# A table of cumulative gates in DRAM: from one row per chunk and head to one row per direction and head

## The chip, the cores and the metric

The kernel runs on one core of a Trainium2 chip. Its time is the device time of one execution in microseconds, taken as the median of several runs. All data are float32 in DRAM; the matrix products of the projections run on float32r pairs of a high and a low part.

## The reference, cut to what matters

One hybrid layer: a bidirectional gated DeltaNet token mixer on 512 latent tokens with a prefix of 256 context tokens, then a mixture of 16 experts with 64 tokens each. Per head and direction the mixer needs the cumulative sum of the log gates within a chunk. It stands in the decay between two tokens of a chunk and in the decay of the query:

```python
gcum = jnp.cumsum(g, axis=-1)                       # (B, H, n, CHUNK)
diff = gcum[..., :, None] - gcum[..., None, :]
decay = jnp.where(incl, jnp.exp(jnp.where(incl, diff, 0.0)), 0.0)
a_low = jnp.where(strict, jnp.einsum('bhnid,bhnjd->bhnij', k_beta, k) * decay, 0.0)
sol = lax.linalg.triangular_solve(a_low + eye, rhs, lower=True, unit_diagonal=True)
att = jnp.einsum('bhnid,bhnjd->bhnij', q, k) * decay
q_dec = q * jnp.exp(gcum)[..., None]
...                                                 # scan over chunks, S_t = a_t (I - b_t k_t k_t^T) S_{t-1} + b_t k_t v_t^T
```

The kernel takes chunks of 128 tokens: 2 of context and 4 of latents, 6 in all, with 8 heads of 128 columns and 2 directions.

## The kernel before, in words

The program has two stages. In the first, up to about 630 us, PE computes the projections of head after head (lines 141 to 143, three products for each float32 one) and between them the small products of the DeltaNet heads. In the second it streams the weights of the 16 experts through a ring of buffers (`w`, line 636) and multiplies them with the tokens (lines 1580 and 1561).

The first stage is planned by hand: generators ask for an engine and a duration (`Ask`), the function `run` picks the next of them by its own reckoning of free times, and the instructions are recorded in that order. Each engine then runs its instructions strictly in the recorded order. `dma(nbytes, at)` is the planner's price of a transfer, and takes no account of how a transfer is cut. All loads and stores are issued by SP and share one queue over the 16 DMA engines, so a transfer waits for those issued before it.

`gates` computes the cumulative log gates of all heads at once. They are transposed to `gr`, 96 rows (direction, chunk, head) of 128 tokens, and stored to the table `grow_d` in DRAM (line 1022). From there each head reads rows back, with every row repeated over all 128 partitions:

- `head_a` (line 1060) loads one `ff` tile per direction, 6 chunks of 128 values on each partition, 384 KB. The address pattern comes from `grow`. POOL masks the tile (line 1065), ACT takes the exponential (line 105), DVE multiplies it with the products of the keys into `ct` (lines 1116, 1117) and sorts its diagonal blocks (`cd`), which go to DRAM as `bd` (line 1128).
- `invert` reads `bd` back as `lb` (line 1137) and inverts the blocks of 32 by 31 steps of two instructions on POOL (`tb` and `xb`, lines 1148 and 1150). The result goes out as `xd` (line 1153) and comes back as `cr` (line 1158). `head_b` goes on with it on DVE (`cx`, lines 1217 and 1218) and PE (line 1227 and after). Masks for a later head stand in the middle of these steps.
- `decay_q` (line 1290) loads one `qa` tile per direction, 4 latent chunks, 256 KB. ACT takes the exponential, POOL multiplies it with the queries (line 1298), and the scan's output product reads it (line 1348).

On the same engines run the short convolutions (DVE, line 283), the splitting of weights (ACT line 299, DVE and POOL line 303, from `wt<-in_win`, line 136), and the modulation: pieces `e<-in_wm` (line 344) that POOL, ACT and DVE reduce (lines 355 to 375) and PE sums up (lines 382 and 396). At the start the bias rows `gtm` (line 807) and `gtf` (line 809) are loaded in the same repeated manner from a row of `in_brow`.

The address pattern of the repeated loads before:

```python
def grow(d, h, c):
    return bass.AP(tensor=grow_d.tensor, offset=grow_d.offset + ((d * NCH + c) * H + h) * C,
                   ap=[[0, P], [H * C, NCH - c], [1, C]])
```

Of the kernel before, what the change touches and what calls it, by code (L numbers as in the profile page):

```python
# [11 lines left out]
F32 = mybir.dt.float32  # L12
# [7 lines left out]
P = 128  # L20
# [5 lines left out]
H = 8  # L26
C = 128
NC_CTX = CTX // C
NC_LAT = SEQ // C
NCH = NC_CTX + NC_LAT  # L30
# [19 lines left out]
def gdn_moe_kernel(ctx: ExitStack, tc: tile.TileContext, a, out):  # L50
# [889 lines left out]
    for b in range(2):  # L940
        for d in range(2):
# [3 lines left out]
    gt = qa[:, NCH * P:NCH * P + 4 * NCH * H].rearrange("p (c d t h) -> p c d t h", c=NCH, d=2, t=2)  # L945
    gc, gs, neg, egt = (ua[:, xw + i:xw + i + 2 * NCH * H].rearrange("p (d c h) -> p d c h", d=2, c=NCH)
                        for i in range(0, 8 * NCH * H, 2 * NCH * H))
    grow_d = tc.dram_tile([2 * NCH * H, C], F32, name="grow_d")

    def gates():  # L950
        abT = gp.tile([64, TOK], F32, tag="ff0_0", bufs=1, name="abT")
# [67 lines left out]
        v.tensor_copy(gr, pr)  # L1019
        give(sl, t2)  # L1020
        t2 = yield Ask("D", 0.5, t2)
        sy.dma_start(grow_d, gr)
        done["G", 0] = dma(1 << 16, t2)
        t = yield Ask("A", 0.4, t, table="exp")
        act("exp", neg, gc, AF.Exp)
# [17 lines left out]
        return pt  # L1043

    def grow(d, h, c):
        return bass.AP(tensor=grow_d.tensor, offset=grow_d.offset + ((d * NCH + c) * H + h) * C,
                       ap=[[0, P], [H * C, NCH - c], [1, C]])

    HALF = (range(0, 4), range(4, 6))

    def head_a(h):
# [5 lines left out]
        for d in range(2):  # L1057
            tf = yield Ask("D", 0.5, lambda: fin(("G", 0), ("T", h - 2)))
            f_ = head_tile(f"ff{d}_", h, [P, NCH, C])
            sy.dma_start(f_, grow(d, h, 0))  # L1060
            tf = dma(3 << 17, tf)
            ff.append(f_)
            sg = 1 if d == 0 else -1
            tf = yield Ask("G", 0.85, tf)
            g.affine_select(out=f_, in_=f_, pattern=[[0, NCH], [sg, C]], compare_op=OP.is_ge, fill=-1e30,
                            base=0, channel_multiplier=-sg)
# [215 lines left out]
    def decay_q(h):  # L1282
        x = hd[h]
        x["qd"] = []
        qds = qa[:, 1024:].rearrange("p (d t) -> p d t", d=2)
        t0 = []
        for d in range(2):
            t = yield Ask("D", 0.5, lambda: fin(("S0", h - 1), ("S1", h - 1)))
            qd = qds[:, d]
            sy.dma_start(qd.rearrange("p (c i) -> p c i", c=NC_LAT), grow(d, h, NC_CTX))  # L1290
            x["qd"].append(qd)
            t0.append(dma(1 << 18, t))
        for d in range(2):
            qd = x["qd"][d]
            t = yield Ask("A", av(SEQ), t0[d], table="exp")
            act("exp", qd, qd, AF.Exp)
            t = yield Ask("G", 1.25, lambda: None if fin(("q", h)) is None else max(t, fin(("q", h))))
            g.tensor_mul(qd, qd, x["q"])
            done[f"D{d}", h] = t
# [451 lines left out]
```

## Time and profile before

| | us |
|---|---|
| median of 3 runs | 1574.14 |
| lowest and highest | 1568.88, 1575.66 |
| the profiled execution, its own time | 1573.24 |
| its span, from the first to the last instruction | 1571.5 |

The profile is of one execution. A span is the time from the first to the last instruction; what lies around it is 1.7 us. The windows give the busy time of each engine in a stretch, the granted clock of PE and the busy share of the 16 DMA engines. The timeline gives one engine's instructions in order; in brackets stands how long the engine was idle ahead of one, and whose end released it. The chain of waits follows the program back from its last instruction.

### The profile page before, as it was taken

What the parts mean: (1) busy time and instruction counts of PE and PEld (TensorE: products, weight loads), DVE (VectorE), ACT (ScalarE), POOL (GpSimd) and SP (SyncE); (2) the same over time, 40 slices, a digit from 0 to 9 for tenths busy, and PEclk for the clock granted to TensorE, in tenths of its full rate; (3) what the DMA queues carried; (4) which work ended last, traced back from release to release, by engine and by line L of the source; (5) the groups of instructions that cost most, each with busy time, mean ns of one, the idle gap of its engine ahead of it and who ended that gap; (6) DMA issues with size and microseconds to landing.
All of it is one profiled execution on the core that took longest, in us unless ns stands there. A gap on an engine that the chain in (4) does not pass through costs nothing.

```text
span 1571.5 us, 20699 instructions
## 1 busy us (share of the span) xinstructions
PE 1374.7 (87%) x8058; PEld 752.6 (48%) x8058; DVE 721.5 (46%) x1545; ACT 405.3 (26%) x1038; POOL 381.0 (24%) x645
## 2 busy tenths in 40 slices
PE   5889898988986889999999989889889899899867
PEld 1677687766875766433434324224223323324314
DVE  7779896977995896222222222222222222222103
ACT  3356474655574533000000000000000000000012
POOL 2548866857657830000000000000000000000001
PEclk8889999999998999999999999999999999999979
DMA  8145443443453566899999999999999999999992
GB/s 347 54 135 142 135 114 91 117 130 95 133 122 72 205 243 248 364 426 426 425 426 425 425 426 426 427 425 425 426 425 426 426 425 426 425 426 426 425 426 109
DMA packets 112515, 480.12 MB, mean 306 GB/s; under 512 B 45505, under 2 KB 66209, under 8 KB 81826
## 3 DMA queue, kind: packets, MB, share of 16 engines
q1 hardware_dynamic: 112418, 478.81, 77.9%
q8 instruction: 63, 1.03, 0.3%
q14 instruction: 34, 0.28, 0.1%
HBM read 471.92 MB, written 6.86 MB: 305 GB/s over the span
## 4 chain that ended last, share of the span: by engine, by line
DMA 48%; PE 26%; DVE 14%; POOL 8%; issue 2%; ACT 1%; SPq 0%; DVEq 0%; POOLq 0%; ACTq 0%
DMA w<-in_wgu 25%; DMA w<-in_wd 13%; PE gu L1580 10%; PE dn L1561 4%; POOL xb L1150 3%; POOL tb L1148 3%; DMA cr<-xd 2%; DVE e L375 2%; PE gc L1561 2%; PE gc L1511 2%; DMA fg<-in_fg 1%; DVE wl L303 1%; DMA ff__690<-grow_d 1%; DMA ff__1139<-grow_d 1%; PE gc L1548 1%
## 5 line engine op out<-in xcount | busy, mean ns | idle before, releaser
L1580 PE MATMUL gu<-w,xsT 128*64 128x512 f32 x2044 | 472.9, 606 | 32.4 <-DMA w<-in_wgu 31.6
L1580 PEld LDWEIGHTS gu<-w,xsT 128*64 128x64 f32 x2044 | 138.4, 138 | 291.5 <-issue 239.4
L1667 POOL TENSOR_TENSOR hres<-acc,fg 128x256 f32<-128x256 f32 (+1 forms) x6 | 6.0, 1004 | 953.1 <-DVE acc L1655 953.0
L1561 PE MATMUL dn<-w,work 128*64 128x512 f32 x896 | 202.0, 600 | 25.2 <-DMA w<-in_wd 25.2
L1550 DVE TENSOR_TENSOR acc<-gc,acc 128x512 f32<-128x512 f32 x104 | 70.7, 690 | 299.5 <-PE gc L1548 299.5
L141 PE MATMUL pp<-uh,wh 128*128 128x512 f32 (+1 forms) x368 | 153.4, 417 | 1.7 <-ACT cz L265 1.7
L143 PE MATMUL pp<-uh,wl 128*128 128x512 f32 (+1 forms) x368 | 138.9, 377 | 3.8 <-DVE wl L303 2.9
L142 PE MATMUL pp<-ul,wh 128*128 128x512 f32 (+1 forms) x368 | 137.9, 375 | 0.0
L1561 PEld LDWEIGHTS dn<-w,work 128*64 128x64 f32 x896 | 62.4, 137 | 154.2 <-issue 116.8
L1148 POOL TENSOR_TENSOR tb<-lb,xb 96x126 f32<-96x126 f32 (+22 forms) x248 | 118.3, 477 | 65.8 <-DMA lb<-bd 48.6
L1150 POOL TENSOR_TENSOR xb<-xb,tb 96x126 f32<-96x126 f32 (+22 forms) x248 | 125.1, 504 | 19.4
L1532 ACT ACTIVATE work<-tr 128x512 f32<-128x512 f32 x14 | 8.4, 597 | 423.1 <-PE tr L1525 423.1
L1512 DVE TENSOR_SCALAR xsT<-gc,ffn 128x128 f32<-128x128 f32 x64 | 26.2, 410 | 154.1 <-PE gc L1511 154.1
L1542 ACT CAST yh<-work 64x512 fp32r<-64x512 f32 x28 | 17.3, 617 | 253.1 <-DVE work L1539 252.8
L143 PEld LDWEIGHTS pp<-uh,wl 128*128 128x128 f32 x368 | 74.7, 203 | 16.1 <-DVE wl L303 3.3
L141 PEld LDWEIGHTS pp<-uh,wh 128*128 128x128 f32 x368 | 75.1, 204 | 10.7 <-ACT cz L265 2.2
L142 PEld LDWEIGHTS pp<-ul,wh 128*128 128x128 f32 x368 | 75.3, 205 | 6.3
L1511 PEld LDWEIGHTS gc<-oneh,hres 128*128 128x128 f32 x512 | 64.5, 191 | 20.2 <-issue 18.3
L1511 PE MATMUL gc<-oneh,hres 128*128 128x128 f32 x512 | 69.2, 280 | 0.4 <-DVE oneh L1504 0.4
L375 DVE SCALAR_TENSOR_TENSOR e<-e,cs,e 128x128 f32<-128x128 f32 x133 | 66.0, 512 | 1.8
L1613 DVE TENSOR_TENSOR work<-gu,work 128x512 f32<-128x512 f32 x32 | 22.0, 692 | 80.9 <-PE gu L1580 79.7
L1548 PEld LDWEIGHTS gc<-yh,pgt 128*128 128x128 f32 x112 | 19.8, 186 | 82.0 <-issue 68.2
(443 smaller groups left out, 2042.7 us busy)
## 6 DMA issues: line engine op xcount, KB each, us to landing
w<-in_wgu SPq DMA_DIRECT2D x100, 2048.0 KB, 34.3
w<-in_wd SPq DMA_DIRECT2D x45, 2048.0 KB, 34.3
w<-in_wgu SPq DMA_DIRECT2D x55, 1024.0 KB, 31.9
w<-in_wd SPq DMA_DIRECT2D x22, 1024.0 KB, 31.8
e<-in_wm SPq DMA_DIRECT2D x32, 512.0 KB, 4.4
wt<-in_win SPq DMA_DIRECT2D x31, 512.0 KB, 4.6
w<-in_wdt SPq DMA_DIRECT2D x6, 2048.0 KB, 30.7
wm<-in_wm SPq DMA_DIRECT2D x3, 2048.0 KB, 14.6
```

The lines of the kernel that those rows point to most:

```text
L141: pe.matmul(pp, wh[:, k, :], uh[i][:, k, :], start=k == 0, stop=False)
L142: pe.matmul(pp, wh[:, k, :], ul[i][:, k, :], start=False, stop=False)
L143: pe.matmul(pp, wl[:, k, :], uh[i][:, k, :], start=False, stop=k == KT - 1)
L375: v.scalar_tensor_tensor(acc, wm[:, k], cs1[:, k, 0:1], acc, op0=OP.mult, op1=OP.add)
L1148: g.tensor_tensor(t_, lb[:, k + 1:, k:k + 1].to_broadcast([2 * NB, m, n_]), xb[:, k:k + 1, 0:n_].to_broadcast([2 * NB, m, n_]), OP.mult)
L1150: g.tensor_tensor(xb[:, k + 1:, 0:n_], xb[:, k + 1:, 0:n_], t_, OP.subtract)
L1511: pe.matmul(pg, hres[:, t, k * P:k * P + P], oneh[:, t].rearrange("p a b -> p (a b)"), start=t == 0, stop=t == NC_LAT - 1)
L1512: v.tensor_scalar(xsT[:, k, :], pg, ffn[:, 0, k:k + 1], ffn[:, 1, k:k + 1], op0=OP.mult, op1=OP.add)
L1548: pe.matmul(pcb, pgt[:, t, :], yh[:, dh], start=True, stop=True)
L1550: v.tensor_add(acc[t // 2][:, t % 2, cs], pcb, hres[:, t, cs] if first else acc[t // 2][:, t % 2, cs])
L1561: pe.matmul(pd[64 * g_:64 * g_ + 64], hs_[g_][i][:, cb, 64 * j:64 * j + 64], wcols(w, c0, w_), start=ft == 0, stop=ft == 15, tile_position ...
L1580: pe.matmul(gu[m][f // 2][hs], xsT[:, k, es], wcols(w, 2048 * m + 512 * f, 512), start=k == 0, stop=k == KT - 1, tile_position=(0, 64 * (f ...
```

## The change

The table gets one row per direction and head, with the six chunks of that head side by side, 3 KB. The rows of a head for the latent chunks are then the last 2 KB of the same row. So each partition of an `ff` load reads one run of 3 KB, where it read six of 512 B that lay 4 KB apart; each partition of a `qa` load reads one run of 2 KB instead of four of 512 B. Bytes, loads and destinations stay as they are. The store is cut into two, one for each direction, with runs of 512 B as before.

```diff
-    grow_d = tc.dram_tile([2 * NCH * H, C], F32, name="grow_d")
+    grow_d = tc.dram_tile([2 * H, NCH * C], F32, name="grow_d")
...
-        sy.dma_start(grow_d, gr)
+        for d in range(2):
+            sy.dma_start(grow_d[d * H:(d + 1) * H].rearrange("h (c i) -> c h i", c=NCH), gr[d * NCH * H:(d + 1) * NCH * H])
...
     def grow(d, h, c):
-        return bass.AP(tensor=grow_d.tensor, offset=grow_d.offset + ((d * NCH + c) * H + h) * C,
-                       ap=[[0, P], [H * C, NCH - c], [1, C]])
+
+        return bass.AP(tensor=grow_d.tensor, offset=grow_d.offset + ((d * H + h) * NCH + c) * C,
+                       ap=[[0, P], [1, (NCH - c) * C]])
...
-            sy.dma_start(f_, grow(d, h, 0))
+            sy.dma_start(f_.rearrange("p c i -> p (c i)"), grow(d, h, 0))
...
-            sy.dma_start(qd.rearrange("p (c i) -> p c i", c=NC_LAT), grow(d, h, NC_CTX))
+            sy.dma_start(qd, grow(d, h, NC_CTX))
```

The instructions of PE, DVE, ACT and POOL stand in the same order before and after. SP has one row more. On SP at the store and the first loads of the table (`wt` are projection weights, `e` modulation weights), before:

```order
L136 DMA wt<-in_win 128x1024
L1022 DMA grow_d<-gr 96x128
L344 DMA e_454<-in_wm 128x1024
L1060 DMA ff__660<-grow_d 128x6x128
L1060 DMA ff__690<-grow_d 128x6x128
L136 DMA wt<-in_win 128x1024
```

And the same place on SP now:

```order
L136 DMA wt<-in_win 128x1024
L1023 DMA grow_d<-gr 6x8x128 x2
L344 DMA e_454<-in_wm 128x1024
L1062 DMA ff__661<-grow_d 128x768
L1062 DMA ff__691<-grow_d 128x768
L136 DMA wt<-in_win 128x1024
```

A second store stands ahead of the same loads. The first `ff` load waits for the first store, the second for the second.

On SP near the end of the stage, where `cr`, the result of an inversion, is read behind a pair of `qa` loads, before:

```order
L1153 DMA xd_5226<-xb 96x512
L1128 DMA bd_5234<-cd 128x12x32
L136 DMA wt<-in_win 128x1024
L1290 DMA qa<-grow_d 128x4x128 x2
L1158 DMA cr<-xd_5226 128x24x16
L1137 DMA lb<-bd_5234 48x1024 x2
```

And the same place on SP now:

```order
L1155 DMA xd_5227<-xb 96x512
L1130 DMA bd_5235<-cd 128x12x32
L136 DMA wt<-in_win 128x1024
L1292 DMA qa<-grow_d 128x512 x2
L1160 DMA cr<-xd_5227 128x24x16
L1139 DMA lb<-bd_5235 48x1024 x2
```

Nothing has moved there; the two `qa` loads have one run on each partition in place of four.

## Rows read from the trace of the kernel before

**Rows 1.** Windows: start:end, length, busy of the engines, PE clock, DMA share, GB/s.

```profile
33.00:39.00 6.00, 6.00 (x25) 3.11 (x29) 4.11 (x14) 1.75 (x4) 3.29 (x4) 0.51 0.62 212
83.00:88.00 5.00, 5.00 (x28) 4.23 (x27) 4.93 (x5) 2.95 (x8) 1.88 (x1) 1.00 0.24 69
56.00:500.00 444.00, 379.68 (x2897) 320.16 (x2895) 361.16 (x781) 259.90 (x725) 302.88 (x527) 0.92 0.44 114
590.00:635.00 45.00, 42.36 (x276) 28.38 (x275) 30.64 (x88) 15.31 (x41) 0.24 (x1) 1.00 0.58 219
635.00:1571.00 936.00, 841.84 (x4046) 323.38 (x4045) 216.62 (x429) 70.39 (x140) 5.98 (x6) 0.98 0.98 412
```

**Rows 2.** Chain that ended last, first stage: start us, us, what.

```profile
80.13 14.25 DMA ff__690<-grow_d
...
324.23 11.22 DMA e<-in_wm
...
343.52 13.12 DMA ff__3654<-grow_d
...
493.16 11.10 DMA cr<-xd
```

**Rows 3.** DMA issues up to 640 us: KB each, median us to landing.

```profile
e<-in_wm SPq DMA_DIRECT2D x32, 512.0 KB, 4.4
...
cr<-xd SPq DMA_DIRECT2D x8, 192.0 KB, 4.1
...
gtm<-in_brow SPq DMA_DIRECT2D x1, 512.0 KB, 19.7
...
gtf<-in_brow SPq DMA_DIRECT2D x2, 128.0 KB, 12.6
```

**Rows 4.** Timeline of PE, idle time in brackets.

```profile
97.98 0.59 PE L382 MATMUL pq<-ones,e 128*128 128x1 f32 x2 [4.34 <-POOL e L367]
...
165.02 1.05 PE L1227 MATMUL pq<-cx,ct 32*32 32x32 f32 x48 [3.50 <-DVE cx L1218]
...
265.26 0.58 PE L382 MATMUL pq<-ones,e 128*128 128x1 f32 x2 [4.37 <-POOL e L367]
...
335.37 0.39 PE L141 MATMUL pp<-uh,wh 128*128 128x256 f32 x1 [1.73 <-ACT cz L265]
...
341.88 0.37 PE L1274 MATMUL pq<-ua,y 64*64 64x64 f32 x1 [1.98 <-DVE wa L1385]
...
380.77 0.31 PE L1227 MATMUL pq<-cx,ct 32*32 32x32 f32 x2 [5.53 <-DVE cx L1218]
...
433.75 0.72 PE L1227 MATMUL pq<-cx,ct 32*32 32x32 f32 x48 [1.40 <-DVE cx L1218]
...
505.60 0.98 PE L1227 MATMUL pq<-cx,ct 32*32 32x32 f32 x48 [8.46 <-DVE cx L1218]
```

**Rows 5.** Timeline of POOL, the masks of the loaded tiles.

```profile
94.50 0.86 POOL L1065 TENSOR_SCALAR_AFFINE_SELECT ff__690<-ff__690 128x768 f32<-128x768 f32 x1 [5.05 <-DMA ff__690<-grow_d]
...
138.28 1.15 POOL L1065 TENSOR_SCALAR_AFFINE_SELECT ff__1139<-ff__1139 128x768 f32<-128x768 f32 x1 [1.24 <-DMA ff__1139<-grow_d]
...
240.47 0.87 POOL L1065 TENSOR_SCALAR_AFFINE_SELECT ff__2316<-ff__2316 128x768 f32<-128x768 f32 x1 [1.26 <-DMA ff__2316<-grow_d]
...
244.19 0.86 POOL L1065 TENSOR_SCALAR_AFFINE_SELECT ff__2373<-ff__2373 128x768 f32<-128x768 f32 x1 [1.94 <-DMA ff__2373<-grow_d]
...
356.70 0.86 POOL L1065 TENSOR_SCALAR_AFFINE_SELECT ff__3654<-ff__3654 128x768 f32<-128x768 f32 x1 [5.54 <-DMA ff__3654<-grow_d]
...
419.92 0.87 POOL L1065 TENSOR_SCALAR_AFFINE_SELECT ff__4343<-ff__4343 128x768 f32<-128x768 f32 x1 [2.49 <-DMA ff__4343<-grow_d]
```

**Rows 6.** Timeline of DVE, two waits.

```profile
335.48 0.80 DVE L373 TENSOR_SCALAR e<-e,cs 128x128 f32<-128x128 f32 x1 [3.60 <-DMA e<-in_wm]
...
379.79 0.52 DVE L1217 COPY cx<-cr 128x96 f32<-128x96 f32 x2 [6.38 <-DMA cr<-xd]
```

**Rows 7.** Line 1022, the store's issue: duration ns min/median/max, first and last start us.

```profile
L1022 SPq DMA_DIRECT2D grow_d<-gr x1: 341/341/341, 78.1 to 78.1; - x1
```

## The prediction

> **What bounds the kernel now.** First the windows by stage. From 635 us to the end the kernel only streams expert weights: the DMA engines are 98% busy at 412 GB/s, so that stage lasts as long as its bytes take [rows 1]. The change touches nothing in it. Just before it, from 590 to 635 us, the DMA share is 0.58: the ring of weight buffers fills with time to spare, so whatever brings the first gate-and-up matmul forward brings the end forward by as much [rows 1]. The gain has to be found before 545 us, in the DeltaNet stage.
>
> There no engine is the bound by itself: in the 444 us from 56 to 500, PE is busy 379.7 us and DVE 361.2 [rows 1]. What is left, 64 us of idle PE, is all that waits can give back there. So the second view is the chain that ended last: broadcasts of the table stand on it, for 14.25 and 13.12 us at two of their places, and twice another DMA that was issued behind a pair of them, `e<-in_wm` with 11.22 us and `cr<-xd` with 11.10 [rows 2]. A `cr<-xd` takes 4.1 us at the median, an `e<-in_wm` 4.4 [rows 3]; the rest was the queue.
>
> Why is a broadcast of 384 KB so long? From 83 to 88 us the two loads of the first head have the queue nearly to themselves. It moves 69 GB/s, and the 16 engines are busy 24% of that time [rows 1]. They are starved, not full. It isn't the making of descriptors either: `cr<-xd` writes 128x24 runs of 64 B, 3072 runs, in 4.1 us, some 750 a us [rows 3], against 69 GB/s / 512 B = 135 runs a us here. What is special is that all engines read the same few rows of 512 B.
>
> Last come the waits of PE, POOL and DVE, engine by engine, since the sum is made there.
>
> **The change part by part.**
>
> *Speed of a broadcast.* No trace shows one of 3 KB runs. The nearest rows are the broadcasts of the modulation bias at the start, `gtm` (runs of 4 KB, 512 KB) and two `gtf` (2 KB, 128 KB each): 768 KB, each load read by all its partitions from one row [rows 3]. They pass between 33 and 39 us together with one 512 KB weight load, 212 GB/s over 6 us [rows 1]. If they needed the whole 6 us, 0.786 MB / 6 = 131 GB/s. If the weight load took its own 0.524 MB / 412 GB/s = 1.3 us apart (412 is the rate of the last stage [rows 1]), 0.786 / 4.7 = 167 GB/s. I take 148, near the middle, because 3 KB lies between 2 and 4. The far ends are 69 GB/s (the run's length changes nothing) and 412 (line rate). So 0.393 MB goes from 5.7 us to 2.7, 3.0 saved, and 6.0 for the second of a pair; the `qa` load (0.262 MB) goes from 3.8 to 1.8, 2.0 saved, 4.0 for a pair.
>
> The Trainium skill ("DMA: Bandwidth & Descriptors", section "Why small descriptors are slow (HBM only)") speaks against this: a packet costs about three extra cycles on top of one per 32 bytes. By that, 512 B runs already go at 16/19 of line rate, and an estimate by that page is under 0.2 us saved per broadcast and no change of the time. The trace doesn't agree: 69 GB/s with the engines busy 24% [rows 1].
>
> *The places where the chain passes.* Of each I count what PE gets back, which is the smaller of what the load saves and what PE stood idle.
>
> 1. Loads of head 0. POOL waits 5.05 us for `ff__690` at 94.50; its next products feed the matmul for which PE stands 4.34 us at 97.98 [rows 4, 5]. That load comes 6.0 us earlier, so all **4.3** go. Next late there is the convolution on DVE.
> 2. Loads of head 1, in the middle of head 0's inversion. The inversion begins 4.3 us earlier by place 1. POOL's wait for `ff__1139`, 1.24 us, goes too; PE idles 3.50 us at 165.02 for its result [rows 4, 5]. **1.2**.
> 3. Loads of head 3. POOL waits 1.26 and 1.94 us (240.47, 244.19); PE then stands 4.37 us at 265.26 for POOL [rows 4, 5]. **3.2**.
> 4. `e<-in_wm` behind a pair of `qa` at 324. DVE waits 3.60 us for it, and PE idles 1.73 + 1.98 us (335.37, 341.88) after that [rows 4, 6]. The pair saves 4.0; PE gets **3.4**, a little under DVE's 3.60.
> 5. Loads of head 5. POOL waits 5.54 us at 356.70 for the second, which lands 6.0 earlier, and the inversion goes on. DVE waits 6.38 us for its result and PE 5.53 [rows 4 to 6]. **5.5**.
> 6. Loads of head 6. POOL's wait of 2.49 us at 419.92 goes; PE's is 1.40 us at 433.75 [rows 4, 5]. **1.4**.
> 7. `cr<-xd` behind a pair of `qa` at 493: 4.0 earlier, of PE's 8.46 us at 505.60 [rows 2, 4]. **4.0**; what remains is the weight load ahead of it in the queue.
> 8. The other loads (`ff` of heads 2, 4 and 7, the remaining `qa`): I find no idle PE behind them. **0**. What hides them is POOL's inversion and PE's projections; with those gone they would be worth 3.0 us for an `ff` and 2.0 for a `qa`.
>
> Sum: 4.3 + 1.2 + 3.2 + 3.4 + 5.5 + 1.4 + 4.0 = 23.0 us.
>
> *The store.* One DMA of 48 KB becomes two. The second is one more issue on SP, 0.34 us as the first was [rows 7], ahead of an `e` load and both `ff` loads; queued behind it are only loads, and its landing is waited for by the second `ff` load alone. Bounds 0 and 1 us, once: nothing if SP stands waiting for the landing anyway, three issues' time if the halves land that much later. I take **0.4**, next to the row of the issue.
>
> *The order.* PE, DVE, ACT and POOL keep their rows. ACT and DVE get waits on loads that POOL has waited for already, so they are met when they are reached: 0. If POOL's select didn't stand ahead of them, they would bind as POOL's waits do now.
>
> Net 22.6 us. The profiled execution took 1573.24 us, of which 1571.5 is the span; 1573.2 - 22.6 = 1550.6. The median of the runs is 0.9 us higher: **1551**. With 131 or 167 GB/s instead of 148 each place moves by less than 1 us; at 412 GB/s only places 4 and 7 could gain more. The figure hangs less on the rate than on PE's idle time.
>
> **The rivals.**
>
> *A: run length is not the limit.* All engines still read one small row, and the rate stays at 69 GB/s. For it: the engines are idle three quarters of the time now, so nothing that they do per packet sets the pace [rows 1]. Then 1573.2 + 0.9 + 0.4, about 1574. Against it: the bias rows, read in the same way, went at 131 GB/s or more. The packet rule of the Trainium skill's DMA page gives A's time by another road.
>
> *B: the saved time is handed back.* PE gets these matmuls earlier, but the convolutions and scans on DVE (361 of 444 us busy) don't follow, and a wait of PE for DVE grows [rows 1]. For it: DVE has no more room than PE has. Against: DVE's own long waits (6.38 us at 379.79, 3.60 at 335.48) lie at the same places, so it moves with PE [rows 6]. With half of the sum lost: 1574 - 11 = 1563.
>
> *C: more than the sum.* The rate is nearer to 412 GB/s, or the weight loads behind broadcasts, which I left at nothing, land earlier where ACT waits for them: 32 to 36 us, about 1540.
>
> *D: slower.* Long runs make all engines walk one 3 KB row in step, each blocking the others, where today a load's six pieces lie 4 KB apart. Its places are those above. At 50 GB/s an `ff` load takes 7.9 us instead of 5.7, a pair 4.4 longer, a `qa` pair 2.9: 4.4 + 4.4 + 4.4 + 2.9 + 4.4 + 2.2 + 2.9 = 25.6 us for places 1 to 7, about 1600. It decides from 69 GB/s downwards. Against it: the same bias rows.
>
> **How the numbers follow.** What a measurement of this kernel can tell from no change is about 0.5%, 7.9 us, so faster means below 1566. Forecast (1543 to 1558) 0.52, B (1559 to 1566) 0.17, C (below 1543) 0.08, A (1567 to 1577) 0.17, D 0.06. Faster 0.52 + 0.17 + 0.08 = 0.77, same 0.17, slower 0.06. The range may leave out 0.2: from 1538, which cuts half of C (0.04), to 1572, which cuts 0.10 of A and all of D.
>
> **What would show it.** In the profile after, plain microseconds of a broadcast should carry 131 to 167 GB/s, and the second `ff` of a pair should land some 7 us after its issue instead of 13 to 14. If they still carry 69, A is right and all else falls. POOL's six waits for these loads (17.5 us together [rows 5]) should nearly vanish, the two rows `cr` and `e` of the chain should fall to some 7 us, and PE's idle time from 56 to 500 us should fall from 64 to about 45. If the loads are faster but PE's idle time isn't less, B is right. The weight stage should be as long as it is, 936 us, only earlier; if it grows, the ring was not full when it began, and passing the gain on one for one was wrong.

## The result: about 1% faster, 13 to 17 us of the 22.6 forecast

The changed kernel takes 1555.57 us (median of 5 runs, 1552.06 to 1559.34), the kernel before, on the same chip, 1568.88 (5 runs, 1566.07 to 1575.66). These two medians lie 13.3 us apart. The ratio on record, which isn't their quotient, is 0.9893, with a 95% interval of 0.9872 to 0.9913: 17 us less, give or take 3. The forecast was 22.6 us less. The profiled execution has a span of 1557.6 us, 13.9 less than that of before.

**The broadcasts.** They did become fast. The issue view (KB each, median us to landing) answers to [rows 3]; `ff__691` is the load that took 14.25 us in [rows 2]:

```profile
qa<-grow_d SPq DMA_DIRECT2D x16, 256.0 KB, 4.9
cr<-xd SPq DMA_DIRECT2D x8, 192.0 KB, 3.8
ff__661<-grow_d SPq DMA_DIRECT2D x1, 384.0 KB, 4.6
ff__691<-grow_d SPq DMA_DIRECT2D x1, 384.0 KB, 5.2
```

Before, the `qa` loads took 8.6 us at the median, and the first two `ff` loads 8.8 and 14.3. The windows (columns as in [rows 1]) show the stage, the weight stage, and the first pair of `ff` loads with an `e` load beside it:

```profile
56.00:500.00 444.00, 383.16 (x3072) 323.08 (x3071) 391.38 (x809) 269.31 (x746) 317.08 (x554) 0.94 0.40 119
620.50:1556.50 936.00, 842.51 (x4048) 323.57 (x4047) 216.74 (x430) 70.39 (x140) 5.97 (x6) 0.98 0.98 413
81.00:84.00 3.00, 3.00 (x15) 2.49 (x14) 2.47 (x2) 1.53 (x3) 1.58 (x1) 1.00 0.99 286
```

The DMA engines are full (0.99) where they stood at 0.24 [rows 1]. The weight stage begins 14 us earlier, and the program ends 13.9 earlier, so what is gained ahead of that stage passes through one for one. But DVE is now busy 391.4 of the 444 us from 56 to 500, where it was busy 361.2 [rows 1]. Part of that is work pulled in from later; part isn't.

PE's idle time in that window was a sign that the prediction named: it should fall from 64 us to about 45. It is 60.8 us (444 less 383.2), but 175 more matmuls fall into the window. Windows with the same number of instructions compare better: the changed kernel up to 484.5 us has the 2897 matmuls and the 781 DVE instructions of [rows 1], and the last two lines, before and changed, end where the weight stage begins:

```profile
56.00:484.50 428.50, 371.54 (x2897) 313.59 (x2895) 377.90 (x781) 261.43 (x728) 304.27 (x528) 0.95 0.40 119
56.00:635.00 579.00, 495.85 (x3818) 409.01 (x3816) 466.46 (x1021) 315.11 (x863) 357.41 (x612) 0.93 0.48 138
56.00:620.90 564.90, 492.92 (x3818) 407.45 (x3816) 482.57 (x1021) 314.52 (x863) 356.64 (x612) 0.95 0.45 141
```

For the same 2897 matmuls PE idles 57.0 us where it idled 64.3, and is busy 371.5 us where it was busy 379.7, at a mean granted clock of 0.95 in place of 0.92. Up to the weight stage, 11.2 of the 14.1 us gained are idle time and 2.9 are busy time. So PE got back half of the idle time that the forecast counted, and the rest of the gain is a term that its sum doesn't have. How firm that rest is can't be said from one execution of each: PE's busy time in the whole program is 1374.7 us in the kernel before and 1371.2 in the one-add form of it below, which takes the same time.

The busy times of the whole program:

```profile
PE 1371.8 (88%) x8058; PEld 751.0 (48%) x8058; DVE 737.6 (47%) x1545; ACT 404.8 (26%) x1038; POOL 380.3 (24%) x645
```

In the kernel before the page of the profile has 721.5 us for DVE: the same 1545 instructions take 16.1 us longer, and nothing in them was changed. All of it lies between 56 us and the weight stage (482.6 and 466.5 above). Here the missing time begins.

**The waits.** POOL's waits for `ff` loads are down to two (they answer to [rows 5]; line, what ended them, us, times, longest):

```profile
POOL ff__3597 L1067 <- DMA ff__3597<-grow_d: 1.0, 1, 1.0
POOL ff__3655 L1067 <- DMA ff__3655<-grow_d: 0.9, 1, 0.9
```

PE's timeline, idle time in brackets, answers to [rows 4]:

```profile
115.43 1.11 PE L1043 MATMUL pq<-ident,cv 128*128 128x128 f32 x4 [3.71 <-ACT cv L105]
...
136.31 0.38 PE L382 MATMUL pq<-ones,e 128*128 128x1 f32 x2 [3.19 <-DVE e L375]
...
329.86 0.36 PE L1276 MATMUL pq<-ua,y 64*64 64x64 f32 x1 [2.18 <-DVE wa L1387]
...
363.81 1.22 PE L1335 MATMUL sc<-Vs,ktok 128*128 128x128 f32 x4 [5.09 <-DVE vx L1332]
...
486.32 0.98 PE L1229 MATMUL pq<-cx,ct 32*32 32x32 f32 x48 [3.77 <-DVE cx L1220]
...
525.61 0.71 PE L1335 MATMUL sc<-Vs,ktok 128*128 128x128 f32 x4 [3.67 <-DVE vx L1332]
```

The waits of 4.34, 3.50, 4.37 and 5.53 us that the forecast counted on are gone, and the one of 8.46 us is 3.77. Of the two behind the late `e`, 1.73 us went, and the 1.98 us for DVE's `wa` stayed (2.18 at 329.86). In their place stand new ones: 3.71 us for ACT and 3.19 for DVE early, 5.09 for DVE at 363.81, 3.67 for DVE at 525.61.

**Where it was gained and lost.** Each head's inversion ends with SP's issue of the `xd` store. These times (us, from SP's timeline) show how far ahead the changed kernel is; the last row is a weight load just ahead of the weight stage.

| up to | before | changed | ahead | gained in this stretch | forecast there |
|---|---|---|---|---|---|
| `xd` of head 0 | 157.5 | 155.0 | 2.5 | 2.5 | 5.5 (places 1, 2) |
| head 1 | 202.9 | 199.9 | 3.0 | 0.5 | 0 |
| head 2 | 262.7 | 252.8 | 9.9 | 6.9 | 3.2 (place 3) |
| head 3 | 314.5 | 302.4 | 12.1 | 2.2 | 0 |
| head 4 | 373.9 | 354.9 | 19.0 | 6.9 | 8.9 (places 4, 5) |
| head 5 | 424.6 | 409.1 | 15.5 | -3.5 | 1.4 (place 6) |
| head 6 | 490.2 | 474.7 | 15.5 | 0 | 0 |
| head 7 | 550.6 | 533.5 | 17.1 | 1.6 | 4.0 (place 7) |
| `w<-in_wgu` | 637.7 | 623.6 | 14.1 | -3.0 | 0 |

The kernel is 19 us ahead at 355 us and loses five of them again.

**What stands at 355 us.** DVE's timeline first, then POOL's at the same time (start us, us, engine, line, operation):

```profile
356.05 5.41 DVE L1118 TENSOR_TENSOR ct<-ff__3597,ff__3655 128x256 f32<-128x256 f32 x1
```
```profile
354.89 1.04 POOL L355 TENSOR_TENSOR e<-e,cs 128x512 f32<-128x512 f32 x1
355.89 1.28 POOL L364 TENSOR_TENSOR e<-e 128x512 f32<-128x512 f32 x1
...
360.45 0.72 POOL L364 TENSOR_TENSOR e<-e 128x256 f32<-128x256 f32 x1
361.25 0.52 POOL L367 TENSOR_TENSOR e<-e 128x128 f32<-128x128 f32 x1
```

An add of 128x256 takes 5.41 us, from just after the start of POOL's streak (two pieces of the modulation, back to back) nearly to its end (361.46 against 361.77). In the kernel before the same add came ahead of that streak:

```profile
367.59 0.42 DVE L1116 TENSOR_TENSOR ct<-ff__3596,ff__3654 128x256 f32<-128x256 f32 x1
```

There POOL's streak ran from 373.9 to 380.6, while DVE stood in the very wait of 6.38 us for `cr` [rows 6] that the forecast meant to win back. The wait had covered the streak. The kernel before isn't free of such meetings, though: at 133.35 one `e` of DVE takes 3.83 us (some 0.5 elsewhere) while POOL runs two `qa` products and a mask. In the changed kernel, where POOL no longer waits for the second mask, another `e` takes 4.72 us at 131.10, across the two products and both masks. A second long hold that is new is `ol<-os,oh` at 520.94: 4.42 us for an instruction that takes 0.68 elsewhere, beside three `wot` products of POOL (3.71 us), with PE's wait of 3.67 us behind it. Both stand on the chain of work that ended last (start us, us, what):

```profile
356.13 5.33 DVE ct L1118
...
477.54 7.86 DMA cr<-xd
521.02 4.34 DVE ol L766
```

No load of the table is among its 55 longest pieces any more; `cr` at 477.54 answers to the 11.10 us in [rows 2].

### The profile page after: what moved, and what is told of

Its sections match the earlier page's. It is cut to its first block, busy times and chain, and to the rows that moved or that the text cites. A ratio compares the mean times of both kernels' runs of the same rounds, so it can differ in the third digit from the quotient of the medians.

```text
span 1557.6 us, 20697 instructions
## 1 busy us (share of the span) xinstructions
PE 1371.8 (88%) x8058; PEld 751.0 (48%) x8058; DVE 737.6 (47%) x1545; ACT 404.8 (26%) x1038; POOL 380.3 (24%) x645
## 4 chain that ended last, share of the span: by engine, by line
DMA 40%; PE 32%; DVE 16%; POOL 7%; ACT 2%; issue 2%; SPq 0%; DVEq 0%; POOLq 0%; ACTq 0%
DMA w<-in_wgu 23%; DMA w<-in_wd 13%; PE gu L1582 12%; PE dn L1563 4%; POOL tb L1150 3%; POOL xb L1152 3%; PE gc L1513 2%; PE gc L1563 2%; DVE e L375 2%; DMA cr<-xd 2%; DMA fg<-in_fg 1%; DVE cv L283 1%; DVE wl L303 1%; PE gc L1550 1%; PE pp L141 1%
## 5 line engine op out<-in xcount | busy, mean ns | idle before, releaser
L1582 PE MATMUL gu<-w,xsT 128*64 128x512 f32 x2044 | 473.0, 606 | 32.4 <-DMA w<-in_wgu 31.8
L1152 POOL TENSOR_TENSOR xb<-xb,tb 96x126 f32<-96x126 f32 (+22 forms) x248 | 118.2, 477 | 19.4
L375 DVE SCALAR_TENSOR_TENSOR e<-e,cs,e 128x128 f32<-128x128 f32 x133 | 69.8, 540 | 1.8
```

Source lines behind the costliest of these rows:

```text
L375: v.scalar_tensor_tensor(acc, wm[:, k], cs1[:, k, 0:1], acc, op0=OP.mult, op1=OP.add)
L1152: g.tensor_tensor(xb[:, k + 1:, 0:n_], xb[:, k + 1:, 0:n_], t_, OP.subtract)
L1582: pe.matmul(gu[m][f // 2][hs], xsT[:, k, es], wcols(w, 2048 * m + 512 * f, 512), start=k == 0, stop=k == KT - 1, tile_position=(0, 64 * (f ...
```

## The experiments

Two questions are open. Why was the old broadcast slow, if the length of its runs was only my guess? And is the lost time due to DVE and POOL meeting, or was DVE next late whatever POOL does? "Theory T" below is that DVE is kept out while POOL computes, "rival N" that DVE is next late in any case. Ratios are to runs of the kernel before on the same chip.

### Why the old broadcast was slow

**A probe of broadcasts**, each load alone (`rd` reads the weights in DRAM; the second list of each access pattern steps over the runs), and of DVE beside POOL:

```
+load(p4k,    rd([[0, P], [1024, 6], [1, 128]]))      # as the old table
+load(p640,   rd([[0, P], [160, 6], [1, 128]]))
+load(run1k,  rd([[0, P], [1024, 3], [1, 256]]))
+load(run1p5k, rd([[0, P], [1024, 2], [1, 384]]))
+load(run3k,  rd([[0, P], [1, 768]]))
+load(own512, rd([[8192, P], [1024, 6], [1, 128]]))
...
+for i in range(5): gpsimd.tensor_tensor(bo[i], big[i], sc, mult)   # POOL, 128x512
+for i in range(3): vector.tensor_add(do[i], da, db)                # DVE, 128x256
```

> A probe that computes nothing of the reference: only (a) eight forms of a broadcast load, four times each, every one alone (it is issued when the one before has been read), from the weights in DRAM, and (b) short streaks of POOL products 128x512 with three DVE instructions beside them. (a) Forms of 384 KB: 6 runs of 512 B at 4 KB pitch (the old table), the same at 640 B pitch, 3 runs of 1 KB, 2 runs of 1.5 KB, one run of 3 KB (and of 2 KB, 256 KB), and 512 B runs and 3 KB runs of which every partition reads its own. If the run's length sets the pace, all three forms of 512 B runs are slow (about 7.2 us to landing, the fastest ff of before), and 1 KB and 1.5 KB lie between that and the 3.8 us of the fastest ff of the changed kernel. If it is the 4 KB pitch, the 640 B pitch lands in about 4 us. If it is that all partitions read one place, 512 B runs of their own land in about 4 us, and 3 KB read by all is no better than its own. (b) Theory T, the lock: an add of two SBUF inputs takes 0.42 us alone; beside a streak of POOL's products one of the three is held until the streak ends, 3 us or more, and an instruction with one input or one of its two in PSUM isn't held. Rival E, even sharing: each of the three takes about twice its time, and none over 1.5 us.

Issue view (KB each, median us to landing); `p` is the 640 B pitch, `own` the 512 B runs of which each partition reads its own:

```profile
p4k<-in_wgu SPq DMA_DIRECT2D x4, 384.0 KB, 6.7
p<-in_wgu SPq DMA_DIRECT2D x4, 384.0 KB, 3.5
run3k<-in_wgu SPq DMA_DIRECT2D x4, 384.0 KB, 3.4
own<-in_wgu SPq DMA_DIRECT2D x4, 384.0 KB, 3.3
...
run1k<-in_wgu SPq DMA_DIRECT2D x4, 384.0 KB, 4.5
```

Runs of 512 B are as fast as one of 3 KB when they lie 640 B apart, and also at 4 KB pitch when each partition reads its own. The slow case needs both: a pitch of 4 KB, and all partitions at the same few rows. The runs' length isn't the cause (1 KB at 4 KB pitch lies between, 1.5 KB takes 3.5 us, and 3 KB that each partition has for itself 3.3). The DVE half missed what Theory T expected: beside five products each of the three adds took 1.2 to 1.3 us, and none was held until the streak's end (the rows stand in the last section).

**A second probe** varied the pitch alone (same form of load, 6 runs of 512 B), and put POOL's streak of 355 us, in place, beside single DVE adds:

```
+for pitch in (160, 256, 512, 768, 1024, 1280, 2048):
+    load(f, rd([[0, P], [pitch, 6], [1, 128]]))
+prod(wa, 0); fold(wb, 4); prod(wa, 1); fold(wa, 4); fold(wb, 2); ...   # POOL
+vector.tensor_add(do, da, db)                                          # DVE
```

> A second probe that computes nothing of the reference: (a) broadcasts of 6 runs of 512 B, one at a time, four times each, with pitches of 640 B, 1, 2, 3, 4, 5 and 8 KB between the runs; (b) POOL's streak as it stands at 355 us in the changed kernel (product 128x512, fold 128x512, product, folds 128x512 and 128x256, and so on, in place), with a DVE add of two SBUF inputs beside it. (a) Theory P (powers of two of 4 KB or more put the runs in one place of DRAM): 640 B to 3 KB and 5 KB land in about 3.5 us, 4 KB and 8 KB in 6.5 us or more. Rival S (the further apart, the slower): landing grows with the pitch, 5 KB no faster than 4 KB. (b) Theory T: one add of 0.42 us that starts inside the streak is held until the streak's end, 4 us or more. Rival U (each add waits for the one POOL instruction that runs when it comes, as the first probe's three adds in 3.5 us suggest): no add over 1.9 us, and the 5.41 us of the changed kernel needs something else beside it.

```profile
p<-in_wgu SPq DMA_DIRECT2D x4, 384.0 KB, 3.6
p1k<-in_wgu SPq DMA_DIRECT2D x4, 384.0 KB, 3.8
p2k<-in_wgu SPq DMA_DIRECT2D x4, 384.0 KB, 5.0
p3k<-in_wgu SPq DMA_DIRECT2D x4, 384.0 KB, 3.7
p4k<-in_wgu SPq DMA_DIRECT2D x4, 384.0 KB, 6.8
p5k<-in_wgu SPq DMA_DIRECT2D x4, 384.0 KB, 3.3
p8k<-in_wgu SPq DMA_DIRECT2D x4, 384.0 KB, 11.2
```

It isn't distance either: 3 KB and 5 KB are fast, while 2, 4 and 8 KB take 5.0, 6.8 and 11.2 us. Theory P holds (and starts already at 2 KB, lower than expected). The Trainium skill ("DMA: Bandwidth & Descriptors", section "Latency and other measured facts") tells of a like loss for copies whose partitions lie 2 MiB or more apart (164 GB/s at 2 MiB, 207 at 512 KiB), calls its cause an inference, and advises to pad the pitch by a few KiB. The runs here agree on the direction and find it at far smaller pitches, for one small table that all partitions read; 1 KB more between the pieces was enough. What the pitch does inside the memory no run here shows. Part (b) went against Theory T again: beside the streak or its parts an add of 128x256 took 1.0 to 1.4 us, 0.42 alone, as rival U had it.

**The old kernel with padded rows**, in which nothing else is changed:

```
-    grow_d = tc.dram_tile([2 * NCH * H, C], F32, name="grow_d")
+    grow_d = tc.dram_tile([2 * NCH * H, 160], F32, name="grow_d")
-        sy.dma_start(grow_d, gr)
+        sy.dma_start(grow_d[:, :C], gr)
-        return bass.AP(... ((d * NCH + c) * H + h) * C,   ap=[[0, P], [H * C, NCH - c], [1, C]])
+        return bass.AP(... ((d * NCH + c) * H + h) * 160, ap=[[0, P], [H * 160, NCH - c], [1, C]])
```

> The kernel before with one thing changed: a row of its table takes 640 B instead of 512 B, so that the pieces of 512 B that a broadcast reads lie 5 KB apart and not 4 KB. Their length, their number and the order of the rows stay, and so does the single store. In the probe 512 B runs landed in 6.7 us at 4 KB pitch, in 3.5 us at 640 B pitch, and 3 KB runs in 3.4 us. Theory P (the pitch of 4 KB makes the old broadcast slow): this is as fast as the changed kernel or 1 us better, 1553 to 1556 us, with the ff loads landing in 3.8 to 4.6 us. Rival R (the length of the run, as the prediction had it; the probe's 640 B form is fast only because its six runs lie next to each other): the time of the kernel before, 1569 to 1572 us, and ff loads in 7 us or more.

Measured: 1554.4 us, ratio 0.9879 (0.9859 to 0.9898), and `ff` loads that land in 3.8 to 7.5 us, most in 4 to 5.6, a little later than expected. This is Theory P, with the old runs of 512 B and one store. The padding alone, 128 B a row, gains as much as the new layout (0.9893) within the intervals.

### The parts of the change

**`ff` alone, and `qa` alone.** The table is written twice, and either kind of load reads the new layout:

```
+    grow_o = tc.dram_tile([2 * NCH * H, C], F32, name="grow_o")
+        sy.dma_start(grow_o, gr)
-            sy.dma_start(qd, grow(d, h, NC_CTX))
+            sy.dma_start(qd.rearrange("p (c i) -> p c i", c=NC_LAT), grow_old(d, h, NC_CTX))
```

> The change for the ff loads alone: the table is written twice, in the new layout for ff and in the old one for the decay_q loads (one more store of 48 KB, 0.34 us of issue). By the prediction's places 1 to 3, 5 and 6 are the ff loads' and 4 and 7 the qa loads': 15.6 of its 23.0 us. Scaled to the measured 14 to 17 us that would be 9 to 11 us less than before, 1559 to 1562 us. Theory T (half of what the early places gain is lost again to DVE waiting while POOL computes, wherever it comes from): 7 to 12 us, with qa's waits at 324 and 493 back. Rival Q (ff's own gain is handed back in full, and what remains is due to the qa loads): under 4 us, 1567 us or more.

> The change for the decay_q loads alone: the table is written twice, in the new layout for them and in the old one for the ff loads. With ff alone the time was 0.9921 of before and with both 0.9893. If the two parts add up, this is 0.997, about 4 us less than before: 1567 to 1570 us. By the prediction's places 4 and 7 it would be 7.4 us less, 1565. If the qa loads only gain because the ff loads have moved the rest, it is within 1 us of before; if they were behind ff's gain as well, more than 8 us less.

Measured: `ff` alone 1559.98 us, 0.9921 (0.9905 to 0.9937), some 12 us; `qa` alone 1570.62 us, 0.9985 (0.9967 to 1.0003), some 2 us, not told apart from nothing. The prediction gave 15.6 us to `ff` and 7.4 to `qa`. The `qa` run pays for its extra stores, which its expectation didn't price: its first `ff` loads are issued 1.7 us later than before (81.43 and 81.86 us against 79.70 and 80.13), and head 0's `xd` comes 3.0 us later (160.5 against 157.5). From there to the weight stage it gains some 4.4 us, so the 2 us are too little for the `qa` loads. With `qa` alone DVE's wait of 3.60 us for `e` [rows 6] is down to 0.7, and with `ff` alone it stands (3.5 us); yet the inversion behind it ends only 1.3 us earlier with `qa` alone (58.1 us from head 3's `xd` to head 4's, 59.4 before). Place 4 was sized by a wait that had another one close behind it.

**One store instead of two.** One more copy on DVE puts the chunk innermost ahead of the transpose:

```
+        gch = w2[:, :2 * NCH * H]
+        v.tensor_copy(gch.rearrange("p (d h c) -> p d c h", d=2, c=NCH), pg[:, 0])
-        pe.transpose(pr, gc.rearrange("p d c h -> p (d c h)"), ident)
+        pe.transpose(pr, gch, ident)
-        for d in range(2):
-            sy.dma_start(grow_d[d * H:(d + 1) * H].rearrange("h (c i) -> c h i", c=NCH), ...)
+        sy.dma_start(grow_d.rearrange("r (c i) -> (r c) i", c=NCH), gr)
```

> The changed kernel with one store of the table: the cumulative gates are copied once more on DVE with the chunk innermost, so that the transposed tile already has the table's order and goes out as one DMA of 48 KB in place of two. The two issues took 0.74 and 0.84 us against 0.34 us of one. Expected by all theories: SP's issue of the first two ff loads comes 0.6 to 1.2 us earlier, less 0.1 to 0.2 us for the copy, and the time falls by 0 to 1 us, to 1554.6 to 1555.6, too little for the timing to tell; the profile is read for it. If instead the first head's loads are no longer what is waited for, nothing moves behind them.

Measured: 1553.51 us, 0.9885 (0.9861 to 0.991), no difference that the timing can tell. In the trace the two `ff` issues stand 1.57 and 1.95 us behind the start of the store, and 2.21 and 2.93 in the changed kernel: the second store costs the two loads 0.6 and 1.0 us there. The issues themselves are dearer than the single one of 341 ns [rows 7] (ns, min/median/max):

```profile
L1023 SPq DMA_DIRECT2D grow_d<-gr x2: 739/790/842, 78.1 to 79.0; - x2
```

### Where the rest went

**One add for two**, so that head 5's adds are over before POOL's streak, in both kernels:

```
-            v.tensor_add(ct[:, csl], ff[0][:, csl], ff[1][:, csl])
+            if cs[0] == 0:
+                v.tensor_add(ct, ff[0], ff[1])
```

> The changed kernel, with the two adds ff0+ff1 of a head (128x512 and 128x256) made one (128x768) where the first stood. In the changed kernel the second add of head 5 took 5.41 us beside POOL's products of the modulation, and PE then waited 5.09 us. Theory T (the DVE add with two SBUF inputs is kept out while POOL runs its products back to back): the one add of head 5, about 1.0 us, is over before the products start; the waits of 5.41 and 5.09 us go, the xd store of head 6 and the scans behind it come 3 to 5 us earlier, and the time falls from 1555.6 to 1551 to 1553. If another two-input instruction of DVE is caught by the same products instead, the gain is under 2 us, and its row shows it. Rival N (DVE is late there anyway, and the long add only shows its waiting): the time stays within 1 us of 1555.6, and PE waits for DVE at the same place.

> The kernel before with the same edit: one add for two. Its adds took 0.42 us each and none was held. Theory T: nothing to gain, within 1.5 us of the kernel before (eight instructions fewer on DVE, some 0.1 us each at most). Rival N, and a rival by which one add is better whatever stands beside it: the same gain here as in the changed kernel.

Measured: 1557.43 us, 0.991 (0.9887 to 0.9933) in the changed kernel, 1575.03 us, 1.0012 (0.9996 to 1.0028) in the one before: no gain in either. The 3 to 5 us that Theory T had expected didn't come, but its second clause did: another instruction is caught by the same streak. DVE's timeline, PE's, then POOL's:

```profile
357.68 1.00 DVE L1119 TENSOR_TENSOR ct<-ff__3592,ff__3650 128x768 f32<-128x768 f32 x1
...
360.06 0.42 DVE L1120 TENSOR_TENSOR ct<-pq,ct 128x256 f32<-128x256 f32 x1
360.52 4.87 DVE L1127 COPY cd<-ct 32x192 f32<-32x192 f32 x1
```
```profile
367.59 0.80 PE L1336 MATMUL sc<-Vs,ktok 128*128 128x128 f32 x2 [5.06 <-DVE vx L1333]
```
```profile
359.00 1.04 POOL L355 TENSOR_TENSOR e<-e,cs 128x512 f32<-128x512 f32 x1
...
365.36 0.45 POOL L367 TENSOR_TENSOR e<-e 128x128 f32<-128x128 f32 x1
```

The add is over in time (1.00 us). The product `ct<-pq,ct`, which has one input in PSUM, runs inside the streak at its usual 0.42 us. Then the streak catches the next instruction that reads SBUF alone, a copy of 32x192 that takes 0.24 us elsewhere and 4.87 here. PE's wait is as long as before, 5.06 us. The hold belongs to the streak, not to the add. The same edit, made on the padded kernel (its second add of head 5 took 5.42 us):

> The old layout with rows of 640 B (its time was 0.9879 of before), and one add ff0+ff1 for a head in place of two. Its second add of head 5 took 5.42 us beside POOL's streak. Theory T: that hold goes, and the scans behind head 5 come 1 to 4 us earlier; in the changed kernel the same edit took the hold away and brought no time, because the shifted work met other streaks. If that was chance, this is 1550 to 1553 us; if each edit only moves where DVE and POOL meet, it is within 2 us of 1554.

Measured: 1556.75 us, 0.9882 (0.9853 to 0.9911), no gain; here a copy `cd<-ct` takes 5.46 us.

**Without POOL's share of the modulation**, in both kernels; the modulation values are left out:

```
-                    g.tensor_tensor(wm[:, hk], wm[:, hk], cs1[:, hk, 0:1].to_broadcast([P, 4, P]), OP.mult)
-                on.tensor_add(wm[:, :i], wm[:, :i], wm[:, i:2 * i])
+                if en == "V":
+                    on.tensor_add(wm[:, :i], wm[:, :i], wm[:, i:2 * i])
```

> The changed kernel without POOL's share of the modulation: its 12 products 128x512 and the first two adds of each of its pieces are left out (the modulation values are then not the reference's), some 35 us of POOL; the order of all that is left is the same. Goes with the next run, the same in the kernel before. Theory T (the changed kernel loses 5 to 9 us because DVE is kept out by these streaks more than before): DVE's busy time from 56 to 560 us falls by 20 us or more against the changed kernel, none of its instructions is held over 2.5 us before 500 us, and the difference of the two kernels without the products is 18 to 23 us instead of 14 to 17. Rival N (what was lost is lost to the rest of DVE's and ACT's work, which is next late): the difference stays at 13 to 17 us. Rival O (POOL's streaks are what both kernels wait for, so that either is faster without them by the same): both fall by 10 us or more, with the difference as it is.

> The kernel before without POOL's share of the modulation, as in the run above (same work left out). Theory T: DVE's instructions were held little here (busy 408 us from 56 to 560, 437.6 in the changed kernel, with some of the tail's work pulled in), so its time falls by less than that of the changed kernel: by 0 to 8 us, to 1561 to 1569. Rivals N and O: it falls by as much as the changed kernel does.

Measured: 1540.12 us, 0.978 (0.9761 to 0.9799), and 1561.36 us, 0.9921 (0.9904 to 0.9938). At the place of the 5.41 us:

```profile
347.79 0.60 DVE L1118 TENSOR_TENSOR ct<-ff__3573,ff__3631 128x256 f32<-128x256 f32 x1
```

The difference of the two kernels is 0.0141 of the time, 22 us, against 0.0107, 17 us, with the products; each carries some 3 to 4 us of uncertainty, so the timing leans to theory T and doesn't prove it; the spans of the profiled executions differ by 16.1 us (1556.1 and 1540.0) against 13.9. The traces say more. DVE's busy time is now 711.1 and 716.8 us: of the 16.1 us that the changed kernel paid more, 5.7 are left. From the first `bd` store to the weight stage the change is worth 16.5 us (526.6 against 510.1), with the products 10.7 (531.1 against 520.4). At head 4's `xd` it is 12.2 us ahead and loses nothing afterwards: 12.9, 14.2 and 15.9 at heads 5 to 7 and 16.1 at the weight load of the table above. And the stretch from head 4's `bd` to head 5's, in which the 5.41 us lie, takes 49.8 us without the products; it takes 54.7 us in the changed kernel and 54.9 with one add, where only the instruction that was held is another. So the streak costs the chain 4.9 us there. The kernel before takes 58.0 in that stretch with and without the products: there the streak costs nothing. Three parts of the expectations missed. DVE's busy time from 56 to 560 us falls by 6 us (437.6 to 431.6) and not by 20 or more; 37 more instructions fall into that window. One `e` of DVE is still held for 4.07 us, at 125.25, beside `qa` products and masks of POOL, which were not left out. And the kernel before falls by 12 us as well, not by 8 at most. In its profiled run (15.4 us shorter) 10.7 of that are gained before the first `bd` store, at 107 us. The changed kernel gains 6.9 us there. POOL's products hold up the start of either kernel, which is rival O for that stretch; without them the first `bd` stores stand at 95.9 and 96.3 us, and the change gains nothing up to there. On the whole T holds for what was lost after 355 us, and the early stretch (places 1 and 2) is not settled between the theories.

**The products moved to ACT**, on the padded kernel:

```
-    MOD_E = "GGAGVVVVGVBVAVAVVVVVAVGAVVVVBVGV"
+    MOD_E = "AAAAVVVVAVBVAVAVVVVVAVAAVVVVBVAV"
```

> The old layout with rows of 640 B, and the products of the seven modulation pieces that POOL made moved to ACT (the letter A of the table in place of G; POOL keeps the folds): 12 products of 1.04 us off POOL, some 2.4 us a piece on ACT, which is busy 295 of 504 us; the planner puts the rows in another order. Theory T: fewer streaks, DVE's two-input instructions are held less, 2 to 8 us less than 1554. Rival: the ACT work delays the exponentials and casts that the chain needs, and the new order costs as much: 1554 or more.

Measured: 1582.31 us, 1.0051 (1.0027 to 1.0074), slower than the kernel before, as the rival of the expectation had it and worse (it is six pieces that move, not seven). The planner's new order brings head 2's `xd` 8 us ahead of the padded kernel's (243.5 against 251.6) and then head 3's `bd` 22.7 us behind it (274.7 against 252.0); the hold on `ct` comes back at another head (4.2 us at 413.49). The run says nothing of the holds apart, since everything else moved too. Why that stretch is so long wasn't followed further.

## Why the prediction was right or wrong

- **The bound and the place.** Right. The gain came ahead of the weight stage, which moved by what was gained. How it came is right in part only: PE's idle time fell by 11.2 us where 22.6 were forecast, and in the window from 56 to 500 us it is nearer to the sign of rival B (no less idle) than to the forecast's 45 us. That PE's matmuls themselves take less time (2.9 us up to the weight stage, 8.1 for the first 2897 of the window), at a higher mean granted clock, stood in no term of the sum.
- **The speed of a broadcast.** The direction was right and the rate too low: 148 GB/s was taken, while the first pair now runs with the DMA engines full, 286 GB/s together with an `e` load; the second of that pair lands 5.2 us after its issue where some 7 were forecast. The reason was wrong. "All engines read the same few rows of 512 B" is only half of it; the other half, the 4 KB pitch, stood in the code and in rival D's wording, and I read past it. Rival A was right that the run's length isn't the limit, and wrong in its time, 1574, because the new layout takes the pitch away as well. That the loads became fast was luck in this respect: the change that was made for the length of the runs also removed the pitch, which was the cause. The rule that I had taken from the Trainium skill's DMA page there (the packet's cost) agrees with the probe in so far as it knows of no great loss for 512 B runs; it was just not what bound here.
- **Places 1 and 2** (5.5 us forecast, 2.5 measured). PE's 4.34 and 3.50 us went, but "all 4.3 go" named the convolution on DVE as next late and gave it no price. What PE waits for now is ACT's `cv` (3.71 us at 115.43), ahead of which ACT waited 4.67 us for a weight load `wt` (1.16 before), and DVE's `e` (3.19 at 136.31). Head 0's `bd` store is 3.4 us earlier, head 1's 0.1.
- **Place 3** (3.2, measured 6.9). POOL's 3.2 us of waits went as forecast. Most of the other 3.7 are POOL's own: the 62 products and differences of head 2's inversion take 28.5 us where they took 32.4. That their meetings with DVE changed too is my reading and has no run of its own; the forecast had no such term. The groups by line, of before and of the changed kernel (busy us, mean ns, idle before):

```profile
L1148 POOL TENSOR_TENSOR tb<-lb,xb 96x126 f32<-96x126 f32 (+22 forms) x31 | 16.3, 525 | 14.4 <-DMA lb<-bd 12.4
L1150 POOL TENSOR_TENSOR xb<-xb,tb 96x126 f32<-96x126 f32 (+22 forms) x31 | 16.1, 520 | 2.4
```
```profile
L1150 POOL TENSOR_TENSOR tb<-lb,xb 96x126 f32<-96x126 f32 (+22 forms) x31 | 14.9, 479 | 14.7 <-DMA lb<-bd 12.7
L1152 POOL TENSOR_TENSOR xb<-xb,tb 96x126 f32<-96x126 f32 (+22 forms) x31 | 13.6, 438 | 2.4
```

- **Places 4 and 5** (8.9, measured 6.9). Right in mechanism for the most part: the waits for `e`, of POOL for head 5's loads and of PE for `cx` are gone. But of the 3.4 us of place 4, PE's wait of 1.98 for DVE's `wa` is still there. Then the step failed that decided the size. Of the 19 us in hand at head 4, 3.5 were lost by head 5. I counted an idle stretch of DVE (6.38 us) as time to win without asking what another engine did in it: POOL ran a streak that held DVE for 5.41 us once the two met.
- **Places 6 and 7** (5.4, measured 1.6, less 3.0 behind them). `cr` at 477 takes 7.86 us in place of 11.10, so the queue gave its part; then the hold of 4.42 us at 520.94 and SP's 4.3 us behind DVE's `wol` before the last `cr` stand in the way. How much of the 3.0 us is the hold's alone wasn't measured.
- **Place 8** (0, measured 2.2 from head 2's `xd` to head 3's). Head 4's second load, `ff__3017`, stood on the chain of the kernel before with 8.03 us at 294.00, and POOL waited 1.56 us for it in the middle of head 3's inversion. Both are gone. The term was put at nothing because no idle PE was found behind it.
- **The store** (0.4). 0.6 us for the first load and 1.0 for the second, since a store in pieces takes 0.74 to 0.84 us to issue and not 0.34. Inside the bounds given, above the value taken.
- **The order** (0). Right: no wait of DVE or ACT for a `grow_d` load appears on the chain.
- **The rivals.** D fell with the rate. B was the right kind of doubt with too little in it: it spoke of DVE's work in general, and against it put DVE's long waits, which were the cover that the change removed. Without POOL's products the change is worth about 22 us by the timing and 16.1 by the profiled executions, so the meetings of DVE and POOL account for a part of the shortfall at least.
- **The number.** The measured time lies between the forecast and rival B, and that it lies so near is in part luck. Up to head 4 the changed kernel is 19.0 us ahead where the places up to there gave 17.6, but the parts are 3.0 instead of 5.5, 6.9 instead of 3.2, 2.2 instead of 0 and 6.9 instead of 8.9: terms that were too high and terms that were missing made up for each other.

## What to carry to other kernels

Before a transfer is called slow for its small pieces, look at the distance between them: a small table read by all partitions wants another pitch than 2, 4 or 8 KB, and padding the rows did here what the new layout does. A wait that goes doesn't all come back as time: see what is next late behind it, with its price. When a wait is counted as gain, look at what the other engines run during it, POOL and DVE above all: here one wait was what kept the two from meeting. And when one instruction is suddenly ten times as long, move it, and see whether another one behind it in the queue inherits the time; then look for the cause on the other engine.

## What the runs showed of the hardware that was not expected

- Broadcasts of 6 runs of 512 B to 128 partitions: 3.3 to 3.8 us at pitches of 640 B, 1, 3 and 5 KB, but 5.0, 6.8 and 11.2 us at 2, 4 and 8 KB, with nothing else on the queue.
- In the first probe three DVE adds of 128x256 with both inputs in SBUF take 1.08 us alone and 3.52 beside POOL's products; three `tensor_scalar` with one input 0.69 and 3.13; three adds with one input in PSUM 1.07 alone and 1.08 beside (start us, us, three together; the first line stands alone, the last three beside POOL):

```profile
121.53 1.08 DVE L134 TENSOR_TENSOR do<-da,db 128x256 f32<-128x256 f32 x3
...
142.67 3.52 DVE L134 TENSOR_TENSOR do<-da,db 128x256 f32<-128x256 f32 x3
...
162.71 1.08 DVE L138 TENSOR_TENSOR do<-pt,db 128x256 f32<-128x256 f32 x3
168.62 3.13 DVE L142 TENSOR_SCALAR do<-da 128x256 f32<-128x256 f32 x3
```

  This agrees with the Trainium skill ("SBUF — State Buffer", section "Who interferes with whom"): DVE and POOL share one pair of ports as an exclusive lock, which takes in DVE instructions with two SBUF inputs and some with one, and the loser waits for the whole instruction. My expectation that one input goes free fell.
- How long the loser waits differs. In the probes no add was held for more than about one POOL instruction (1.5 us at most with its own time, rival U), also beside the very streak of 355 us. In the kernels one DVE instruction was held through all of that streak: 5.41 us, 5.42 in the padded kernel, 6.01 with `ff` alone, 6.35 with one store. Other streaks of POOL do the same, the kernel before included (timeline of DVE):

```profile
133.35 3.83 DVE L375 SCALAR_TENSOR_TENSOR e<-e,cs,e 128x128 f32<-128x128 f32 x1
```

  The Trainium skill's rule there, one instruction, doesn't cover that. What the kernel has beside it that the probe lacks stays open.
